# First group's four slabs side by side, the weights' bounds a group later, and the first output projection's rows landing in x's old buffer

## The chip, the cores and the metric

One core of a Trainium2 chip runs the whole program. The metric is the device time of one execution in microseconds, the median of several runs. Work is done by TensorE (PE, matrix products into PSUM), VectorE (DVE), ScalarE (ACT) and GpSimd (POOL); SyncE (SP) issues most DMAs, and GpSimd's queue issues some.

## What is computed

A trunk of two layers over 1024 tokens of width 1024. In layer 0 the main branch is a causal pooling in four groups, each with its own window and its own 256 x 256 map; beside it stands an attention into 256 memory tokens. Both are gated, and an output projection, a residual and a layer norm follow. Layer 1 (forgetting attention) is not touched by the change.

```python
def mixer_sublayer(x, mem, w_in, w_mem_kv, w_out, main_fn):
    h = x @ w_in                       # columns [main | mem q | main gate | mem gate]
    ...
    y_main = main_fn(u_main)           # layer 0: pooling, windows 2, 4, 8, 16
    y_mem = memory_attention(q_mem, mem, w_mem_kv)
    y = jnp.concatenate([y_main * jax.nn.silu(g_main), y_mem * jax.nn.silu(g_mem)], axis=-1)
    return y @ w_out
...
    x = layer_norm(ALPHA * x + y, ln_g[layer], ln_b[layer])
...
    # pooling: (trailing mean over the window - the token), then a map per group, then a scale
    mixed = jnp.einsum('bsgc,gcd->bsgd', pm, pool_w)
```

## The kernel before

x lies transposed in SBUF as eight tiles of 128 features by 1024 tokens. Each fp32 number is split in parts: `hi` (ScalarE's cast, fp32r), `lo` (what VectorE leaves of it, bf16) and `top` (a bf16 copy of the high part). A product of two such numbers is three matmuls (`three`): high x high, top x low, low x top. `X.top` is made by GpSimd, one copy per tile.

A *slab* is 128 columns of the input weights times all of x: 8 tiles of x, two halves of the tokens (n) and three parts, so 48 matmuls of 128 x 512. Its weights come in two pieces of 256 KB (`pc` 0 and 1, four tiles of x each). The first two slabs use `Wide` weights, whose low part is fp32r too, so that it can be multiplied with x's high part and needs no `X.top`.

Group 0 of the pooling is what the kernel starts with: slabs 0 and 1 (the pooled channels), then slabs 12 and 13 (their gates), then the group's map (L325, 24 matmuls), then the memory attention, then groups 1 to 3. Before the first weights are there, TensorE runs warm-up products on zeros (L98). `load_first` and `load_x` write the loads of the first weights and of x; `raw` is a ring of four landings for weights, `T` a ring of six tiles of 4 KB per partition, in which x lands and which later holds the pooled channels, the parts of mem and the rows of y. In PSUM, `pj` has two banks, `L` four and `T` two.

Most of the order on each engine is set when the program is built, by a scheduler that places instructions by its own costs; `keep_in_program_order` pins an instruction behind those pinned before it on its engine, and `manual_schedule` keeps TensorE's order as written.

`look_ahead` reads weights of layer 1 ahead of time, only to bound them: GpSimd's queue loads a piece into `W`, and VectorE (the first 12) or ScalarE sums its absolute values into `sums`. It is called every so many matmuls of slabs, 80 pieces in all, in group 0's gates, the memory queries, and groups 1 and 2. `bounds_of_weights` takes the maximum of `sums`, transposes it on TensorE (L297), reduces it on VectorE (L298, L299) and spreads it by a small matmul (L300).

`OutProj.rest` runs the output projection in twelve steps: four pairs of row blocks (sp), and in each three thirds (c = 2, 0, 1) of the 1536 inputs. A step loads a third of y's rows from DRAM (`y0d`, 512 KB) into a `T` tile, splits it into two further `T` tiles, and does 48 matmuls (L617). `lines` is a buffer of 32 KB per partition in the place where x's low and top parts were; the norm uses its rows 9 to 14, and `keep` its rows 5 to 8.

Of the kernel before, what the change touches and what calls it, by code (L numbers as in the profile page):

```python
# [9 lines left out]
F32 = mybir.dt.float32  # L10
F32R = mybir.dt.float32r
BF16 = mybir.dt.bfloat16
# [3 lines left out]
ALU = mybir.AluOpType  # L16
AX = mybir.AxisListType

P = 128
S = 1024  # L20
# [52 lines left out]
def run(units):  # L73
    for _ in units:
        pass
# [3 lines left out]
def trunk_kernel(ctx, tc, x, xT, memT, win, wk, wv0, wv, wmk, wmv, wout, poolw, pscale, lng, lnb, bforget, out):  # L79
# [14 lines left out]
    warm = pool.tile([P, NH], BF16, tag="w", name="warm", bufs=6)  # L94
    nc.vector.memset(warm, 0.0)
    idle = psum.tile([P, NH], F32, tag="L", name="idle", bufs=4)
    for _ in range(9):
        nc.tensor.matmul(idle, warm[:, :P], warm, start=True, stop=True)  # L98

    def nm(tag):  # L100
# [3 lines left out]
    def sb(shape, tag, bufs, dt=F32, where=None):  # L104
        return (where or pool).tile(shape, dt, tag=tag, name=nm(tag), bufs=bufs)
# [7 lines left out]
    def T(shape=(P, S), dt=F32R):  # L113
        return sb(list(shape), "T", 6, dt)
# [67 lines left out]
    def parts_of(make, shape):  # L182
        return Split(make(shape), make([shape[0], 2] + list(shape[1:]), BF16))
# [378 lines left out]
    class OutProj:  # L562
# [70 lines left out]
        def begin(self):  # L633
# [8 lines left out]
            for to, y in tiles:  # L642
                pin(nc.scalar.copy(to.top, y))

        def rest(self, resid, X, dst):
            order = [(sp, c) for sp in range(ST // 2) for c in (2, 0, 1)]
            accs, splits, gb = {}, [24], []
            if self.accs:
                accs[0], order[:6], splits = self.accs, [(0, 0), (1, 2), (0, 1), (1, 0), (1, 1)], [16, 24]
            if X is not None:  # L650
                self.split(splits.pop())

            def loads():

                for v in (lng, lnb):
                    t = sb([P, D], "P", 4)
                    nc.sync.dma_start(t, v[self.l].partition_broadcast(P))
                    gb.append(t)

            for sp, c in order:  # L660
                if c == 2:
                    accs[sp] = self.open((("T", 2), ("pj", 2), ("T", 2), ("L", 4))) if 0 in accs and sp == 1 else self.open()
                if self.begun and (sp, c) == (0, 0):
                    ys = self.begun
                else:
                    src, ys = T([P, 4, 2 * P], F32), parts_of(T, [P, 4, 2 * P])
                    nc.sync.dma_start(src, self.yd[c, :, :, sp * 2 * P : (sp + 1) * 2 * P])
# [63 lines left out]
    X = parts_of(stream, [P, KT, S])  # L731

    def load_x(kt, parts=1):
        r = T(dt=F32)
        for i in range(parts):
            cols = slice(i * S // parts, (i + 1) * S // parts)
            nc.sync.dma_start(r[:, cols], xT[kt, :, cols])
            nc.scalar.copy(X.hi[:, kt, cols], r[:, cols])
            nc.vector.tensor_tensor(X.lo[:, kt, cols], r[:, cols], X.hi[:, kt, cols].bitcast(F32), ALU.subtract)

    x1 = dram.tile([S, D], F32, name="x1")
    y0d = dram.tile([3, P, 4, S], F32, name="y0d")
# [2 lines left out]
    with tc.tile_pool(name="in0", bufs=1) as in0:  # L745

        def bt(shape=(P, S), dt=F32R):
            return sb(list(shape), "B", 8, dt, in0)

        def seen(shape):  # L750
            return sb(shape, "W", 4, F32, in0)

        first = [[], []]

        def load_first(f, pc):
            to, r = Wide(bt([P, 2, 4, P]), wt([P, 4, P], BF16)), raw([P, 4, P])
            nc.sync.dma_start(r, win[0, f, pc])
            hi_lo(to, r)
            first[f].append(to)

        load_first(0, 0)
        load_x(0, 2)
        load_first(1, 0)
        for kt in range(1, 4):
            load_x(kt)
# [12 lines left out]
        nc.vector.tensor_scalar(pschalf, psc, 0.5, None, ALU.mult)  # L778

        def pool_group(g, see=None):  # L780
            w = WINDOWS[g]
            pms = []
            for f in (2 * g, 2 * g + 1):
                u = sb([P, S], "P", 4)
                run(slab(
                    first[f] if g == 0 else win[0, f], X, lambda cols, acc: nc.scalar.copy(u[:, cols], acc),
                    ("L", 4) if f == 1 else ("pj", 2),
                ))
                cur, sh = u, 1
                while sh < w:  # L790
                    nxt = G()
                    nc.vector.tensor_tensor(nxt[:, sh:], cur[:, sh:], cur[:, : S - sh], ALU.add)
# [12 lines left out]
            ys = []  # L805
            for f in (2 * g, 2 * g + 1):
                y = sb([P, S], "Y", 4, F32, in0)
                if g == 0:
                    seeing[0] = see
# [599 lines left out]
```

## Time and profile before

| | us |
|---|---|
| runs shown | 1182.02, 1182.39, 1179.73; median 1182.02 |
| the profiled execution, its own time | 1181.94 |
| its span | 1180.2 |
| TensorE busy | 1160.1 (98%) |
| VectorE, ScalarE, GpSimd busy | 774.3, 677.7, 290.1 |

The span is the time from the first to the last instruction in the trace; the own time has what lies around it. All times in the trace count from the span's start. A busy TensorE may still run at half its clock, so the granted clock is to be read beside the busy time. Several instructions of one form that follow each other stand in one row of the order of time, with their count (x48); what is in brackets is the idle time ahead of the row and the instruction that ended it. A few matmuls are missing from the trace.

### The profile page before, as it was taken

What the parts mean: (1) busy time and instruction counts of PE and PEld (TensorE: products, weight loads), DVE (VectorE), ACT (ScalarE), POOL (GpSimd) and SP (SyncE); (2) the same over time, 40 slices, a digit from 0 to 9 for tenths busy, and PEclk for the clock granted to TensorE, in tenths of its full rate; (3) what the DMA queues carried; (4) which work ended last, traced back from release to release, by engine and by line L of the source; (5) the groups of instructions that cost most, each with busy time, mean ns of one, the idle gap of its engine ahead of it and who ended that gap; (6) DMA issues with size and microseconds to landing.
All of it is one profiled execution on the core that took longest, in us unless ns stands there. A gap on an engine that the chain in (4) does not pass through costs nothing. (4 is left out here: it accounts for less than half of the span.)

```text
span 1180.2 us, 20768 instructions
## 1 busy us (share of the span) xinstructions
PE 1160.1 (98%) x7398; PEld 671.8 (57%) x7445; DVE 774.3 (66%) x1827; ACT 677.7 (57%) x1502; POOL 290.1 (25%) x443
## 2 busy tenths in 40 slices
PE   8999999999999999999999999999999999999997
PEld 5566776555555556555674455555555555455554
DVE  6744675555765556547555877778777787784653
ACT  6478775966563233557521776667666677774120
POOL 3321001310000000000012445555554444760000
PEclk8999999999999999999999999999999999999999
DMA  7576657754375554536474879999999999965430
GB/s 262 169 247 198 160 118 215 227 192 152 89 256 166 155 136 117 143 89 124 94 250 106 174 161 227 209 211 199 195 207 161 185 195 196 236 190 175 149 137 36
DMA packets 286712, 203.96 MB, mean 173 GB/s; under 512 B 225168, under 2 KB 238608, under 8 KB 286608
## 3 DMA queue, kind: packets, MB, share of 16 engines
q1 hardware_dynamic: 279632, 179.49, 62.1%
q0 software_dynamic: 6976, 23.14, 6.1%
q8 instruction: 58, 0.95, 0.3%
q14 instruction: 46, 0.38, 0.1%
HBM read 116.01 MB, written 22.61 MB: 117 GB/s over the span
## 5 line engine op out<-in xcount | busy, mean ns | idle before, releaser
L361 PE MATMUL pj<-A,w 128*128 128x512 f16 (+2 forms) x2827 | 646.4, 383 | 3.9 <-DVE A L965 1.2
L361 PEld LDWEIGHTS <-w 128*128 128x128 f16 (+1 forms) x2560 | 247.1, 98 | 283.3 <-issue 12.4
L1088 ACT ACTIVATE T<-MK,s 128x512 f32<-128x512 f32 x192 | 111.2, 579 | 60.2 <-DVE s L1080 39.3
L1117 DVE SCALAR_TENSOR_TENSOR P<-T,s,P 128x512 f16<-128x512 f32 x192 | 112.3, 613 | 49.1 <-ACT P L1116 49.1
L1116 ACT ACTIVATE P<-T,s 128x512 f16<-128x512 f32 x192 | 103.8, 574 | 61.3 <-ACT T L1088 29.5
L617 PEld LDWEIGHTS <-T 128*128 128x128 bf16 x736 | 70.6, 98 | 88.7 <-issue 4.7
L1054 POOL TENSOR_SCALAR_AFFINE_SELECT raw<-R 128x256 f32<-128x256 f32 (+3 forms) x128 | 59.8, 468 | 191.2 <-DVE s L1080 133.5
L201 DVE TENSOR_TENSOR w<-raw,w 128x512 bf16<-128x512 f32 x74 | 52.5, 710 | 59.8 <-ACT w L200 40.1
L325 PE MATMUL L<-A 128*128 128x512 f16 (+3 forms) x384 | 83.8, 326 | 0.7 <-DVE G L1207 0.6
L558 POOL DMA_DIRECT2D y1d<-V x3 | 1.6, 535 | 334.8 <-DVE V L536 332.3
L361 PEld LDWEIGHTS pj<-A,w 128*128 128x128 f32 x352 | 65.1, 188 | 17.0 <-ACT w L200 1.4
L201 DVE TENSOR_TENSOR T<-T,T 128x1024 bf16<-128x1024 f32 x22 | 26.8, 1219 | 68.2 <-ACT T L200 39.4
L180 POOL TENSOR_TENSOR w<-B,w 128x512 f16<-128x512 f32 x54 | 62.8, 1163 | 4.4
L200 ACT CAST w<-raw 128x512 fp32r<-128x512 f32 x76 | 46.8, 615 | 24.8 <-DMA raw<-in_win_dram 10.9
L325 PEld LDWEIGHTS <-A 128*128 128x128 f16 x384 | 36.4, 98 | 42.6 <-issue 1.2
L200 ACT CAST T<-T 128x1024 fp32r<-128x1024 f32 x22 | 23.0, 1047 | 64.9 <-DMA T<-y1d 32.3
L617 PE MATMUL pj<-B,T 128*128 128x512 bf16 (+1 forms) x194 | 54.2, 385 | 0.2
L617 PE MATMUL L<-B,T 128*128 128x512 bf16 (+1 forms) x183 | 52.1, 393 | 0.2
L202 ACT CAST w<-raw 128x512 bf16<-128x512 f32 x78 | 48.2, 618 | 3.3 <-PE pj L361 1.9
L1080 DVE CUSTOM_DVE_ANT_0 MK<-L,R,scales 128x512 f32<-128x512 f32 x64 | 45.3, 709 | 2.2 <-PE L L325 2.0
L513 ACT ACTIVATE P<-L,s 128x256 f32<-128x256 f32 x64 | 29.5, 472 | 22.9 <-DVE s L510 19.5
L269 ACT ACTIVATE W<-W 128x512 f32<-128x512 f32 (+1 forms) x68 | 42.2, 624 | 0.0
(310 smaller groups left out, 1880.1 us busy)
## 6 DMA issues: line engine op xcount, KB each, us to landing
raw<-in_win_dram SPq DMA_DIRECT2D x66, 256.0 KB, 3.5
W<-in_win_dram POOLq DMA_DIRECT2D x48, 256.0 KB, 4.0
R<-cumd SPq DMA_DIRECT2D x16, 512.0 KB, 4.8
B<-in_win_dram SPq DMA_DIRECT2D x15, 512.0 KB, 5.6
y0d<-Y SPq DMA_DIRECT2D x12, 512.0 KB, 4.0
raw<-in_wout_dram SPq DMA_DIRECT2D x24, 256.0 KB, 2.7
T<-y0d SPq DMA_DIRECT2D x12, 512.0 KB, 4.9
A<-A SPq DMA_DIRECT2D x24, 256.0 KB, 4.0
```

What stands on the lines that cost most here:

```text
L180: pin(nc.gpsimd.tensor_tensor(to.lo, src, to.hi, ALU.subtract))
L200: pin(nc.scalar.copy(to.hi, src))
L201: pin(nc.vector.tensor_tensor(to.lo, src, to.hi.bitcast(F32), ALU.subtract))
L202: pin((top or nc.scalar.copy)(to.top, src))
L325: nc.tensor.matmul(acc, a, b, start=i == 0, stop=i == len(terms) - 1)
L361: nc.tensor.matmul(accs[n], a[:, k, :], b[:, pc * 4 + k, n * NH : (n + 1) * NH], start=seen[n] == 1, stop=seen[n] == 3 * KT,)
L617: nc.tensor.matmul(accs[a][nh], y, w, start=kt == 8 and i == 0, stop=kt == 7 and i == 2,)
L1054: tc.keep_in_program_order(nc.gpsimd.affine_select(C[:, :w], R[:, lo:up], [[-1, w]], ALU.is_ge, -NEG, base=w - P, channel_multiplier=1,))
L1080: tc.keep_in_program_order(nc.vector.tensor_tensor_reduce(p[:, lo:up], lg, rows, unq, top, ALU.add, ALU.min, m[:, n : n + 1]))
L1088: nc.scalar.activation(e, p[:, lo:up], AF.Exp, bias=top, scale=-1.0, accum_out=sums[:, n, hd % 2, i : i + 1],)
L1116: nc.scalar.activation(pair[:, lo:up], e, AF.Copy, scale=r)
L1117: nc.vector.scalar_tensor_tensor(pair[:, L + lo : L + up], e, r, pair[:, lo:up], ALU.mult, ALU.subtract)
```

## The change

Four things. Group 0's four slabs are computed side by side by `first_four`, in an order written out by hand: as a tile of x arrives, the wide products of slabs 0 and 1 and the high products of the gates are done with it; the products with x's low and top parts follow when all of x is there. All eight PSUM banks are used for it. The weight pieces of the gates are loaded between x's tiles, the loads and splits are pinned in that order, and the `top` copies of these weights come behind all of them. `bounds_of_weights` moves from the end of group 2 into group 3, ahead of its map. From the second step on, the first output projection loads y's rows into rows 0 to 3 of `lines` (`landing`) instead of a `T` tile. There are ten warm-up products instead of nine.

```diff
-    for _ in range(9):
+    for _ in range(10):
         nc.tensor.matmul(idle, warm[:, :P], warm, start=True, stop=True)
...
+        def landing(self, sp, c):
+            k = 2 * ((sp + c) % 2)
+            return lines[0][:, k : k + 2, :].bitcast(F32).rearrange("p e (k m) -> p (e k) m", k=4 // 2)
...
-                    src, ys = T([P, 4, 2 * P], F32), parts_of(T, [P, 4, 2 * P])
+                    src = T([P, 4, 2 * P], F32) if X is None or (sp, c) == (0, 2) else self.landing(sp, c)
+                    ys = parts_of(T, [P, 4, 2 * P])
...
-        def load_first(f, pc):
-            to, r = Wide(bt([P, 2, 4, P]), wt([P, 4, P], BF16)), raw([P, 4, P])
-            nc.sync.dma_start(r, win[0, f, pc])
-            hi_lo(to, r)
-            first[f].append(to)
+        def load_first(k, pc):
+            r, pin = raw([P, 4, P]), tc.keep_in_program_order
+            if k < 2:
+                to = Wide(bt([P, 2, 4, P]), wt([P, 4, P], BF16))
+            else:
+                if pc == 0:
+                    splits[k] = bt([P, 2, 4, P]), bt([P, 2, 2, 4, P], BF16)
+                to = Split(*(half[:, pc] for half in splits[k]))
+            pin(nc.sync.dma_start(r, win[0, (0, 1, 12, 13)[k], pc]))
+            pin(nc.scalar.copy(to.hi, r))
+            pin(nc.vector.tensor_tensor(to.lo, r, to.hi.bitcast(F32), ALU.subtract))
+            firsts[k, pc] = to
...
+        def first_four(us, ys, see):
+            tags = (("pj", 2), ("L", 4), ("L", 4), ("T", 2))
...
+            def wide(kt):
+                for k in range(2):
+                    for i in (0, 2):
+                        for n in range(2):
+                            product(k, kt, n, i)
+            def high(k, *kts):
+                for kt in kts:
+                    for n in range(2):
+                        product(k, kt, n, 0)
+            wide(0)
+            wide(1)
+            high(2, 0, 1)
+            for kt in (2, 3):
+                wide(kt)
+                high(2, kt)
+            high(3, 0, 1, 2, 3)
+            wide(4)
+            wide(5)
+            high(2, 4, 5)
+            wide(6)
+            high(2, 6)
+            wide(7)
+            high(2, 7)
+            high(3, 4, 5, 6, 7)
+            for k in range(2):
+                for n in range(2):
+                    for kt in range(KT):
+                        product(k, kt, n, 1)
+            seeing[0] = see
...
+            for k in range(2, 4):
+                for n in range(2):
+                    for i in (1, 2):
+                        for kt in range(KT):
+                            product(k, kt, n, i)
+                            done += 1
+                            if done % 7 == 0:
+                                look_ahead()
 
         load_first(0, 0)
         load_x(0, 2)
         load_first(1, 0)
-        for kt in range(1, 4):
-            load_x(kt)
-        for f in range(2):
-            load_first(f, 1)
-        for kt in range(4, KT):
-            load_x(kt)
+        load_x(1)
+        load_first(2, 0)
+        load_x(2)
+        load_x(3)
+        load_first(3, 0)
+        for k in range(4):
+            load_first(k, 1)
+            load_x(4 + k)
+        for to in firsts.values():
+            tc.keep_in_program_order(nc.scalar.copy(to.top, to.hi.bitcast(F32)))
...
+            if g == 3:
+                bounds_of_weights()
             for d in range(2):
...
-            if g == 2:
-                bounds_of_weights()
```

Three places in the built order show it. The first is TensorE's start, right behind the warm-up products. The names: `pj` and `L` are PSUM banks, `A_110` (before) and `A_111` (after) x's high part, `B` the weights of a slab. Before:

```order
L361 MATMUL pj_202<-A_110,B_118 128x512 [waits Activation_49]
L361 MATMUL pj_207<-A_110,B_118 128x512 [waits Activation_49]
L361 MATMUL L_267<-A_110,B_132 128x512 [waits Activation_49]
L361 MATMUL L_272<-A_110,B_132 128x512
L361 MATMUL pj_202<-A_110,B_118 128x512 [waits Activation_49]
```

After:

```order
L783 MATMUL pj_232<-A_111,B_120 128x512 [waits Activation_49]
L783 MATMUL pj_233<-A_111,B_120 128x512 [waits Activation_49]
L783 MATMUL pj_232<-A_111,B_120 128x512 [waits DVE_49]
L783 MATMUL pj_233<-A_111,B_120 128x512
L783 MATMUL L_234<-A_111,B_133 128x512 [waits Activation_49]
L783 MATMUL L_235<-A_111,B_133 128x512
L783 MATMUL L_234<-A_111,B_133 128x512 [waits DVE_49]
```

The low products of slab 0 with x's tile 0 now stand ahead of slab 1, where only its high ones stood. The second place is SyncE's queue around the first output projection's loads of y (`y0d` is read into a tile, and written from `Y`). Before:

```order
L667 DMA T_3420<-y0d 128x4x256 [waits DMAHW7_49,PE_49]
L583 DMA raw_3375<-in_wout_dram 128x512 [waits DMAHW0_49,DMAHW1_49,DVE_49,Activation_49]
...
L583 DMA raw_3399<-in_wout_dram 128x512 [waits DMAHW5_49,DVE_49,Activation_49]
L657 DMA P_3427<-in_lng_dram 128x1024
...
L822 DMA y0d<-Y_3237 128x1024 [waits DMAHW2_49,DVE_49]
L667 DMA T_3479<-y0d 128x4x256 [waits PE_49]
```

After:

```order
L672 DMA T_3420<-y0d 128x4x256 [waits PE_49]
L583 DMA raw_3375<-in_wout_dram 128x512 [waits DMAHW0_49,DMAHW1_49,DVE_49,Activation_49]
...
L672 DMA A_3341<-y0d 128x4x256 [waits PE_49,Pool_49]
L583 DMA raw_3399<-in_wout_dram 128x512 [waits DMAHW5_49,DVE_49,Activation_49]
L661 DMA P_3427<-in_lng_dram 128x1024
...
L899 DMA y0d<-Y_3225 128x1024 [waits DVE_49]
```

The second load of y (`T_3479` before, `A_3341`, which is `lines`, after) has moved from behind the last store of y to ahead of a weight load. The third place is TensorE around the bounds of the weights. Before, at the end of group 2's map:

```order
L297 MATMUL T_2928<-ident,s_2925 3x128 [waits PE_49]
L361 MATMUL pj_2993<-A_110,w_2988 128x512 [waits DVE_49]
L361 MATMUL pj_2993<-A_110,w_2988 128x512 x3
L361 MATMUL pj_2993<-A_110,w_3000 128x512 [waits Activation_49]
L361 MATMUL pj_2993<-A_110,w_3000 128x512
L300 MATMUL T_2928<-s_2927,ones 128x3 [waits DVE_49]
```

After, ahead of group 3's map:

```order
L297 MATMUL T_3297<-ident,s_3294 3x128 [waits PE_49]
L325 MATMUL L_3306<-T_3056,MK_3151 128x512
...
L325 MATMUL L_3306<-T_3145,MK_3152 128x512
L300 MATMUL T_3297<-s_3296,ones 128x3 [waits DVE_49]
```

The two small products have moved to the start of group 3's map. Elsewhere TensorE's order is the same in both.

More of the change, by code (lines that the diff above doesn't have):

```diff
@@ L733, in load_x @@
     def load_x(kt, parts=1):
-        r = T(dt=F32)
+        r, pin = T(dt=F32), tc.keep_in_program_order
         for i in range(parts):
             cols = slice(i * S // parts, (i + 1) * S // parts)
-            nc.sync.dma_start(r[:, cols], xT[kt, :, cols])
-            nc.scalar.copy(X.hi[:, kt, cols], r[:, cols])
-            nc.vector.tensor_tensor(X.lo[:, kt, cols], r[:, cols], X.hi[:, kt, cols].bitcast(F32), ALU.subtract)
+            pin(nc.sync.dma_start(r[:, cols], xT[kt, :, cols]))
+            pin(nc.scalar.copy(X.hi[:, kt, cols], r[:, cols]))
+            pin(nc.vector.tensor_tensor(X.lo[:, kt, cols], r[:, cols], X.hi[:, kt, cols].bitcast(F32), ALU.subtract))
     x1 = dram.tile([S, D], F32, name="x1")
@@ L751, in seen @@
             return sb(shape, "W", 4, F32, in0)
-        first = [[], []]
-        def load_first(f, pc):
-            to, r = Wide(bt([P, 2, 4, P]), wt([P, 4, P], BF16)), raw([P, 4, P])
-            nc.sync.dma_start(r, win[0, f, pc])
-            hi_lo(to, r)
-            first[f].append(to)
+        firsts, splits = {}, {}
+        def load_first(k, pc):
[10 more added lines that the diff above has]
+            firsts[k, pc] = to
@@ new lines, in first_four, with product @@
+        def first_four(us, ys, see):
+            tags = (("pj", 2), ("L", 4), ("L", 4), ("T", 2))
+            accs = [[ps([P, NH], *tag) for _ in range(2)] for tag in tags]
+            seen_of = {}
+            def product(k, kt, n, i):
+                a, b = three(firsts[k, kt // 4], X)[i]
+                cols = slice(n * NH, (n + 1) * NH)
+                at = seen_of[k, n] = seen_of.get((k, n), 0) + 1
+                nc.tensor.matmul(
+                    accs[k][n], a[:, kt % 4, :], b[:, kt, cols], start=at == 1, stop=at == 3 * KT,
+                )
+                if at == 3 * KT and k < 2:
+                    nc.scalar.copy(us[k][:, cols], accs[k][n])
+                elif at == 3 * KT:
+                    gate(accs[k][n], ys[k - 2][:, cols])
+            def wide(kt):
[27 more added lines that the diff above has]
+            seeing[0] = see
+            done = 0
+            for k in range(2, 4):
[6 more added lines that the diff above has]
+                                look_ahead()
@@ L782, in pool_group @@
             pms = []
-            for f in (2 * g, 2 * g + 1):
[L784 to L788, printed above, removed]
+            us = [sb([P, S], "P", 4) for _ in range(2)] if g == 0 else []
+            ys = [sb([P, S], "Y", 4, F32, in0) for _ in range(2)] if g == 0 else []
+            if g == 0:
+                with tc.manual_schedule(engines={PE}):
+                    first_four(us, ys, see)
+            for f in (2 * g, 2 * g + 1):
+                u = us.pop(0) if g == 0 else sb([P, S], "P", 4)
+                if g:
+                    run(slab(win[0, f], X, lambda cols, acc: nc.scalar.copy(u[:, cols], acc)))
                 cur, sh = u, 1
@@ L804, in pool_group @@
             hi_lo(w2, r)
-            ys = []
-            for f in (2 * g, 2 * g + 1):
+            for f in (2 * g, 2 * g + 1) if g else ():
                 y = sb([P, S], "Y", 4, F32, in0)
-                if g == 0:
-                    seeing[0] = see
                 run(gate_units(win[0, 12 + f], y, X))
                 ys.append(y)
+            if g == 3:
+                bounds_of_weights()
             for d in range(2):
```

## The prediction

> **What bounds the kernel now.** I read the page first: the span, the busy share of each engine, then the waits of TensorE over the whole span, and then the stretches of the start in time.
>
> ```profile
> span 1180.2 us, 20768 instructions
> PE 1160.1 (98%) x7398; PEld 671.8 (57%) x7445; DVE 774.3 (66%) x1827; ACT 677.7 (57%) x1502; POOL 290.1 (25%) x443
> ...
> PE pj L361 <- ACT A L738: 1.3, 2, 1.0
> PE L L361 <- ACT B L200: 1.1, 1, 1.1
> PE L L617 <- ACT T L202: 0.9, 1, 0.9
> ```
>
> TensorE is busy in 98% of the span, so only two things can move the time: its few idle microseconds and the stretches in which it runs slowly. The three waits quoted are those that this change touches first: 1.3 and 1.1 us for x and for weights at the start, 0.9 us in the first output projection (L617). The first group also runs slowly, which busy time hides. Five stretches of 3.41 us, cut where the granted clock changes, show it (columns: busy us and matmuls of TensorE, granted clock, DMA share, GB/s), and below them TensorE in order of time:
>
> ```profile
> 1.39:4.80 3.41, 3.41 (x9) 1.00 0.85 256
> 4.80:8.21 3.41, 1.95 (x6) 1.00 0.98 357
> 8.21:11.62 3.41, 2.43 (x7) 0.50 1.03 408
> 11.62:15.04 3.42, 3.42 (x10) 0.50 1.03 413
> 15.04:18.45 3.41, 3.41 (x17) 1.00 1.02 375
> ...
> 5.45 1.02 PE L361 MATMUL pj<-A,B 128*128 128x512 f32 x2 [0.34 <-ACT A L738]
> 9.28 1.22 PE L361 MATMUL pj<-A,B 128*128 128x512 f32 x2 [0.98 <-ACT A L738]
> 11.15 1.05 PE L361 MATMUL pj<-A,B 128*128 128x512 f32 x2
> 12.00 1.05 PE L361 MATMUL L<-A,B 128*128 128x512 f32 x2
> 55.09 4.20 PE L325 MATMUL L<-T,MK 128*128 128x512 f32 x17
> 60.35 10.90 PE L361 MATMUL pj<-A,w 128*128 128x512 f32 x48
> 71.09 4.08 PE L412 MATMUL pj<-T,w 128*128 128x256 f32 x35
> ```
>
> The reader is to see three things. The slab that starts at 60.35 runs undisturbed: 48 matmuls until 71.09, so 0.224 us each. At the half clock two start every 0.85 us (11.15 to 12.00), so 0.427 us each. And the first group, four slabs of 48 and the 24 matmuls of L325, lasts from 5.45 to 60.35, 54.9 us, where four slabs at 10.74 and the 5.26 from 55.09 to 60.35 make 48.2. So 6.7 us are lost there: 2.1 us to the waits for weights (1.1) and for x's tile 1 (0.98), 5.76 x (1 - 0.224 / 0.427) = 2.7 us to the half clock from 9.28 to 15.04, and the rest to pauses too short to be listed as waits.
>
> **Part 1: four slabs side by side.** What TensorE waits for is ScalarE's cast of what has just landed:
>
> ```profile
> 6.89 0.62 ACT L200 CAST B<-raw 128x512 fp32r<-128x512 f32 x1 [0.98 <-DMA raw<-in_win_dram]
> 8.18 1.04 ACT L738 CAST A<-T 128x1024 fp32r<-128x1024 f32 x1
> 9.46 1.04 ACT L738 CAST A<-T 128x1024 fp32r<-128x1024 f32 x1 [0.24 <-DMA T<-in_xT_dram]
> 10.76 1.05 ACT L738 CAST A<-T 128x1024 fp32r<-128x1024 f32 x1 [0.26 <-DMA T<-in_xT_dram]
> 17.23 1.06 ACT L738 CAST A<-T 128x1024 fp32r<-128x1024 f32 x1 [0.24 <-DMA T<-in_xT_dram]
> 7.54 0.69 DVE L201 TENSOR_TENSOR B<-raw,B 128x512 fp32r<-128x512 f32 x1 [0.82 <-ACT B L200]
> ```
>
> Tiles of x (512 KB) land 1.30 us apart (9.46, 10.76), so a weight piece of 256 KB costs 0.65. The order of the first loads up to x's tile 1 is kept; then four gate pieces come in between, so tile 2 lands at 10.1, tile 3 at 11.4, tile 4 (behind two pieces) at 14.0, and tile 7 at 17.23 + 4 x 0.65 = 19.8. Add 1.05 for each cast.
>
> TensorE then: the first four products of slab 0 start at 5.45 as before and use the gap up to 7.5; slab 1 has its weights at 7.51 and their low part at 8.23; tile 1 is cast at 9.22. By then 8 products are through, and from 9.22 on 184 slab products and 24 of the pooling map are left. At the full clock that is 184 x 0.224 + 5.26 = 46.4 us, the end 55.65. No input is late from here on: tile 2 is first needed 12 products after 9.22 (11.9, at the full clock) and ready at 11.15; tile 3 needed at 14.1 and ready at 12.45; tile 7 needed 70 products after 9.22, at 24.9 or later, ready at 20.9. Every tile now feeds 12 products instead of 8, which is what closes the gap.
>
> The clock is the unknown. In the rows above, the stretch with 1.95 us busy of 3.41 is followed by the half clock, the one with 2.43 us (71%) leaves it there, and only the full one lifts it. After the change 4.80:8.21 holds at most two more products, some 60%, so I let the clock fall at 8.21 again. But 8.21:11.62 is then filled from 8.23 to 9.09 and from 9.22 on, 3.26 us of 3.41, nearer to the full stretch than to 71%: I take it that the clock is back at 11.62. From 9.22 to 11.62 then run 5.6 products instead of 10.7, 1.14 us late: **end 56.8, gain 3.55 us**. Both ends: the clock never falls, 55.65 (gain 4.7); it comes back only at 15.04, 13.6 products instead of 26, 2.77 us late, 58.4 (gain 1.9).
>
> The Trainium skill, "TensorE: Matmul & The Clock Gate", section "Part 1: The HAM clock gate (the "warmup" mystery)", says that the clock halves after an idle window of about 3.4 us, and that the windows are free-running. The trace agrees on the length (8.21 less 4.80) but not on the idleness: the longest wait here is 1.1 us. By the rule as worded the clock would not fall, which is the 55.65 above.
>
> The rest of the part costs nothing on TensorE, for these reasons. The tenth warm-up product runs in the 0.34 us gap before 5.45. Four more pieces add 4 x 0.52 to ScalarE and 4 x 0.6 to VectorE, which both wait for landings there. ScalarE's eight top casts move behind the last landing, 20.9 to 25.1; they are first needed after the 96 high and wide products, at 9.22 + 1.14 + 88 x 0.224 = 30.1. GpSimd's copies of x's top hang on tile 6:
>
> ```profile
> 18.45 1.17 POOL L195 TENSOR_SCALAR s<-A 128x1 f32<-128x1 bf16 x1 [17.09 <-DVE pschalf L778]
> 19.59 4.95 POOL L195 TENSOR_SCALAR A<-A 128x1024 bf16<-128x1024 f32 x4
> 27.45 5.04 POOL L195 TENSOR_SCALAR A<-A 128x1024 bf16<-128x1024 f32 x4
> 27.01 4.59 DVE L792 TENSOR_TENSOR G<-P 128x1023 f32<-128x1023 f32 x1
> 37.85 1.22 DVE L792 TENSOR_TENSOR G<-P 128x1023 f32<-128x1023 f32 x1 [0.61 <-ACT P L786]
> ```
>
> They end 14 us after they start, so at 34.3 if they start at 20.2; the gates want them one by one from 39 on. The pooling sums of VectorE start when slab 0 is out, after 34, so they should take the 1.22 us of the lower row and not the 4.59 us of the upper, which ran beside these copies. Both pooled channels are then split by about 46, and the map wants them at 51.5.
>
> **Part 2: rows of y in x's old buffer.** SyncE's load of the second step waits for a free T, behind weight loads and stores in its queue:
>
> ```profile
> 318.90 9.11 SPq L583 DMA_DIRECT2D raw<-in_wout_dram  x5
> 337.01 0.53 SPq L667 DMA_DIRECT2D T<-y0d  x1
> 335.69 0.62 ACT L200 CAST MK<-raw 128x512 fp32r<-128x512 f32 x1 [1.47 <-DMA raw<-in_wout_dram]
> 343.60 1.04 ACT L200 CAST T<-T 128x1024 fp32r<-128x1024 f32 x1 [1.57 <-DMA T<-y0d]
> 345.65 0.60 PE L617 MATMUL L<-W,T 128*128 128x512 bf16 x2 [0.88 <-ACT T L202]
> ```
>
> The load is issued at 337.01, cast at 343.6, and TensorE stands 0.88 us. With the new buffer it waits only for the last slab's products that read x's low half, and it stands in front of the fifth of the weight loads of the first row, which end at 328.0. Its casts come right behind the weight pair cast from 335.69 on, at about 337 to 339, and TensorE wants them at 344.8. **Gain 0.9** (bounds 0 and 0.9). The later steps share two landings, three steps in a row on one, so a load waits for the casts before it; a step's 48 products take 10.6 us, and a landing of 6.6 us plus 2.2 us of casts fits. No step but the second waits in that stage before the change.
>
> **Part 3: bounds a group later.** Before, the small product L300 waits for VectorE, which has other sums ahead of it:
>
> ```profile
> 285.07 0.27 PE L297 MATMUL T<-ident,s 128*3 128x128 f32 x1
> 287.13 0.38 PE L300 MATMUL T<-s,ones 3*128 3x3 f32 x2 [0.41 <-DVE s L299]
> 286.56 0.27 DVE L298 TENSOR_REDUCE s<-T 3x1 f32<-3x128 f32 x1
> 286.86 0.22 DVE L299 TENSOR_SCALAR s<-ident,s 3x3 f32<-3x3 f32 x1
> ```
>
> Now it stands behind five products of group 3's map, 1.1 us, against 0.27 + 0.22 of VectorE, before that map's own sums. **Gain 0.3** (0 to 0.4). The twelve looks into the weights become nine in group 0; the three others go to group 2's spare places.
>
> **Sum:** 3.55 + 0.9 + 0.3 = 4.75 us. The profiled execution took 1181.94 us (its span and 1.7 us around it), which stands 0.08 below the median of the three runs, 1182.02. So 1181.94 - 4.75 = 1177.2.
>
> **The rivals.** *The clock comes back only at 15.04.* For it: it did in this execution. Then 1.9 + 0.9 + 0.3 = 3.1, and 1178.8. *The clock never falls*, because 4.80:8.21 is busier, or because the boundaries lie elsewhere in another execution: 4.7 + 1.2 = 5.9, and 1176.0. *The change does not do what it says*: the four slabs run, but landings are later than their bytes say (gate pieces wait for the raw ring, whose four slots hang on VectorE), and the out projection still waits. If tile 7 were cast at 28.5 and not 20.9, TensorE, there at 26.0 (70 products after 9.22 and the 1.14 us), would lose 2.5 us of part 1; with nothing from part 2 that leaves 1.05 + 0.3, and 1180.6. Against it: VectorE frees the slot of slab 1's first piece at 8.23 (the row at 7.54), and tile 7 has 5 us to spare.
>
> *On the other side: the weights of the first memory-query slab come too late.* Before, their casts were
>
> ```profile
> 46.94 3.27 SPq L214 DMA_DIRECT2D raw<-in_win_dram  x2
> 54.08 0.62 ACT L200 CAST w<-raw 128x512 fp32r<-128x512 f32 x1 [7.31 <-DMA raw<-in_win_dram]
> 56.11 0.62 ACT L200 CAST w<-raw 128x512 fp32r<-128x512 f32 x1 [0.39 <-DMA raw<-in_win_dram]
> ```
>
> 5.7 us ahead of 60.35. Now TensorE is there at 56.8, and the load waits for the casts of mem, which stand behind those of the pooled channels: I put its issue at 46.5, its cast with the same 7.1 us at 54.2, so 2.6 us are left. Each microsecond beyond that is lost one for one; 7.4 us later than I think the gain is gone, and from 9.7 us on the kernel is slower by 0.2%, 1184.4. It would need VectorE's pooling sums to take 4.59 us each once more.
>
> **How the numbers follow.** A difference under 0.2% (2.4 us) can hardly be told from none here; the three runs shown spread over 2.7 us. Chances: my forecast 0.55; clock back late 0.18; never down 0.10; does not do what it says 0.12; weights late 0.05. The first three are faster by over 0.2%: 0.83. The fourth and a little of the fifth make no difference that can be told, 0.13; the rest of the fifth is slower, 0.04. The range reaches from the best clock, 1176.0 less 0.8 of spread between runs, to the rival of 1180.6 plus 0.6 of the same spread: 1175.2 to 1181.2, and leaves out the late weights and some of the fourth.
>
> **What would show it.** Right: the first slab products back to back from 9.2, clock 1.00 from 11.6, the first matmul of the memory queries (L361) near 56.8; no wait of L617 for a cast of T; no wait at L300. Wrong: the clock at 0.50 up to 15 (part 1's size); waits for x after 9.3 (landings); a wait of L361 for a cast of w near 57 (the weights); pooling sums of 4.6 us on VectorE; L617 waiting still near 340.

## The result and the profile after

The changed kernel takes 1174.86 us at the median of 6 runs (1174.46 to 1175.85). The kernel before, timed beside it, came to 1180.33, and its 68 runs in the whole study have the same median, 1180.33 (1177.80 to 1183.01). Three slow executions of the study (1503.19, 2026.65 and 6931.10 us) are left out of every median. The ratio is 0.995, with a 95% interval of 0.9938 to 0.9963: 5.5 us faster, where 4.75 had been forecast, and 0.34 us below the low end of the range.

The head of the page of the changed kernel, and the first of TensorE's waits over its span (total, times, longest, in us):

```profile
span 1172.9 us, 20813 instructions
PE 1158.6 (99%) x7446; PEld 671.6 (57%) x7446; DVE 770.0 (66%) x1827; ACT 680.0 (58%) x1502; POOL 288.2 (25%) x443
```

```profile
PE pj L783 <- ACT A L743: 1.7, 2, 1.4
```

The waits of L361 for B, of L617 for T and of L300 are gone. The longest wait for x was 1.0 us, for tile 1; it is now 1.4 us, for the second half of x's first tile. The stretches between the possible changes of the clock (busy us and matmuls of TensorE, granted clock, DMA share, GB/s), and below them TensorE in order of time at the start and at the end of the first group:

```profile
5.10:8.51 3.41, 1.97 (x8) 1.00 0.98 348
8.51:11.92 3.41, 3.15 (x13) 1.00 1.03 411
11.92:15.34 3.42, 3.42 (x16) 1.00 1.02 398
```

```profile
5.12 0.58 PE L783 MATMUL pj<-A,B 128*128 128x512 f32 x1
7.14 0.97 PE L783 MATMUL pj<-A,B 128*128 128x512 f32 x3 [1.44 <-ACT A L743]
7.94 1.34 PE L783 MATMUL L<-A,B 128*128 128x512 f32 x4
9.54 1.19 PE L783 MATMUL pj<-A,B 128*128 128x512 f32 x4 [0.26 <-ACT A L743]
10.57 2.02 PE L783 MATMUL L<-A,B 128*128 128x512 f32 x8
...
50.64 4.38 PE L325 MATMUL L<-T,MK 128*128 128x512 f32 x18
...
56.02 10.97 PE L361 MATMUL pj<-A,w 128*128 128x512 f32 x48
```

The granted clock stays at 1.00 after 5.10, though the stretch 5.10:8.51 is hardly busier (1.97 us) than the one of 1.95 us after which it fell before. From 9.54 on products run without a listed wait, and the first memory query starts at 56.02 instead of 60.35. That is 4.33 us of the 7.29 us between the two profiled executions (1181.94 and 1174.65; the first of them stood 1.6 us above its kernel's median). The rest comes later, 1.21 us of it up to the start of the output projection (333.69 and 328.15). The places of the other two parts look like this now:

```profile
322.44 0.27 PE L297 MATMUL T<-ident,s 128*3 128x128 f32 x1
...
323.55 0.38 PE L300 MATMUL T<-s,ones 3*128 3x3 f32 x2
...
320.97 0.53 SPq L672 DMA_DIRECT2D A<-y0d  x1
329.96 1.05 ACT L200 CAST T<-A 128x1024 fp32r<-128x1024 f32 x1
339.00 0.59 PE L617 MATMUL L<-W,T 128*128 128x512 bf16 x2
```

The load of the second step is issued at 320.97, ahead of most of the weight loads, and cast 8 us before L617 reads it. Here the two traces stand 6.65 us apart (345.65 and 339.00).

### The profile page after: what moved, and what is told of

It reads as the page before. It is cut to its first block, busy times and chain, and to the rows that moved or that the text cites. A ratio compares the mean times of both kernels' runs of the same rounds, so it can differ in the third digit from the quotient of the medians.

```text
span 1172.9 us, 20813 instructions
## 1 busy us (share of the span) xinstructions
PE 1158.6 (99%) x7446; PEld 671.6 (57%) x7446; DVE 770.0 (66%) x1827; ACT 680.0 (58%) x1502; POOL 288.2 (25%) x443
## 5 line engine op out<-in xcount | busy, mean ns | idle before, releaser
L361 PE MATMUL pj<-A,w 128*128 128x512 f16 (+2 forms) x2736 | 620.7, 382 | 1.9 <-DVE A L1040 1.0
L361 PEld LDWEIGHTS <-w 128*128 128x128 f16 (+1 forms) x2464 | 238.5, 98 | 270.5 <-issue 7.9
L617 PEld LDWEIGHTS <-T 128*128 128x128 bf16 x736 | 70.6, 98 | 87.5 <-issue 4.1
L201 DVE TENSOR_TENSOR w<-raw,w 128x512 bf16<-128x512 f32 x70 | 48.2, 689 | 51.1 <-ACT w L200 35.4
L361 PEld LDWEIGHTS pj<-A,w 128*128 128x128 f32 x320 | 59.5, 188 | 13.7
L617 PE MATMUL pj<-B,T 128*128 128x512 bf16 (+1 forms) x198 | 54.8, 384 | 0.0
L617 PE MATMUL L<-B,T 128*128 128x512 bf16 (+1 forms) x186 | 52.4, 393 | 0.0
L202 ACT CAST w<-raw 128x512 bf16<-128x512 f32 x70 | 43.4, 620 | 2.9 <-PE pj L361 1.5
L1155 DVE CUSTOM_DVE_ANT_0 MK<-L,raw,s 128x512 f32<-128x512 f32 (+1 forms) x64 | 41.1, 643 | 0.5 <-issue 0.3
L412 PE MATMUL pj<-T,w 128*128 128x256 bf16 (+1 forms) x344 | 41.0, 279 | 0.0
```

Of the source, the lines that this page charges most:

```text
L201: pin(nc.vector.tensor_tensor(to.lo, src, to.hi.bitcast(F32), ALU.subtract))
L202: pin((top or nc.scalar.copy)(to.top, src))
L361: nc.tensor.matmul(accs[n], a[:, k, :], b[:, pc * 4 + k, n * NH : (n + 1) * NH], start=seen[n] == 1, stop=seen[n] == 3 * KT,)
L617: nc.tensor.matmul(accs[a][nh], y, w, start=kt == 8 and i == 0, stop=kt == 7 and i == 2,)
L1155: tc.keep_in_program_order(nc.vector.tensor_tensor_reduce(p[:, lo:up], lg, rows, unq, top, ALU.add, ALU.min, m[:, n : n + 1]))
```

## The experiments

The table sums them up. "Less before" is the median less that of the kernel before in the same set of runs, and "products a tile" are those of slabs 0 and 1 that are done when a tile of x comes. "Products" are TensorE's products of the first group that have started by 15.04 us in the profile (about one record of them is missing from each trace). "Query" is the start of the first memory-query product, all in us.

| kernel | median | less before | products | query |
|---|---|---|---|---|
| before (profile 1) | 1180.33 | 0 | 18 | 60.35 |
| before, profile 2 | | | 16 | 61.33 |
| changed | 1174.86 | -5.47 | 32 | 56.02 |
| first part alone | 1175.29 | -5.13 | 34 | 55.51 |
| landing alone | 1179.53 | -0.89 | 23 | 59.15 |
| bounds alone | 1179.39 | -1.03 | 21 | 59.35 |
| landing and bounds | 1179.20 | -0.47 | 18 | 59.84 |
| before, 20 warm-ups | 1179.95 | -0.47 | 25 | 59.52 |
| changed, 2 warm-ups | 1175.68 | -4.44 | 31 | 56.24 |
| changed, 9 warm-ups | 1175.51 | -4.61 | 29 | 56.67 |
| 8 products a tile, gates behind | 1175.15 | -4.97 | 34 | 55.47 |
| 4 products a tile, gates behind | 1178.28 | -1.84 | 19 | 58.92 |
| 8 products a tile, gates as before | 1179.07 | -0.61 | 32 | 60.08 |

**The first part alone.** The changed kernel without its other two parts:

```
-                    src = T([P, 4, 2 * P], F32) if X is None or (sp, c) == (0, 2) else self.landing(sp, c)
+                    src = T([P, 4, 2 * P], F32)
...
-            if g == 3:
-                bounds_of_weights()
...
+            if g == 2:
+                bounds_of_weights()
```

> The first part alone: four slabs side by side with the tenth warm-up product, while the second step's rows of y land in T as before and the bounds stay at the end of group 2. Theory C (the granted clock, which stayed at 1.00 in the changed kernel, and the gap-free first slabs make the start's gain, and the start makes most of the whole): the first memory-query product starts near 56.0 us instead of 60.35, as in the changed kernel; from the marks of the two traces 4.3 us by the end of group 0 and 5.2 us by group 3, so 1 to 1.5 us slower than the changed kernel, near 1176.2, if the kernel before is at its median of 1180.3. Rival S (the record's split): 3.55 of 4.75 us from this part, the rest from the other two. Rival N (the parts depend on each other: SyncE's queue and the sums of VectorE move together): the marks behind group 3 differ from the changed kernel's by more than the 1.1 us of the out projection and the 0.36 us of the bounds.

Ratio 0.9955 (0.9943 to 0.9968), 1175.29 us. So the first part brings 5.1 us of 5.5, more than theory C's 4.1 and than the prediction's share of 3.55 in 4.75. What the other two add is 0.43 us, less than the spread of either kernel's runs (1.4 and 1.5), so it is not shown to differ from nothing. TensorE's row of the second output step, where rows of y still land in T:

```profile
338.68 0.60 PE L617 MATMUL L<-W,T 128*128 128x512 bf16 x2
```

No wait stands behind it, although its load is issued as late as 329.89: the 0.88 us that the second part was to save is not there in this profile.

**The landing alone and the bounds alone**, each put into the kernel before:

```
+        def landing(self, sp, c):
...
-                    src, ys = T([P, 4, 2 * P], F32), parts_of(T, [P, 4, 2 * P])
+                    src = T([P, 4, 2 * P], F32) if X is None or (sp, c) == (0, 2) else self.landing(sp, c)
```

> The kernel before with the second part alone: rows of y land in x's old buffer instead of T. By the record: 0.9 us faster (0 to 0.9), the wait of L617 for the cast of T gone near 345. By the marks of the two traces: 1.1 us by the first output row and up to 0.5 us more over layer 1 if that later gain hangs on this landing too, so 0.9 to 1.6 us faster than the kernel before. Rival: the first group has to be faster for the load to be issued earlier; then L617 still waits and the time does not move.

```
+            if g == 3:
+                bounds_of_weights()
...
-            if g == 2:
-                bounds_of_weights()
```

> The kernel before with the third part alone: the bounds of the weights are taken inside group 3. By the record 0.3 us faster (0 to 0.4), the wait of L300 at 287 gone. Rival: the sums then wait elsewhere on VectorE and group 3's map starts later by as much, 0. Nothing else may differ, so at the median within 0.5 us of the kernel before.

Ratios 0.9993 (0.9985 to 1.0002) and 0.9991 (0.9982 to 1.0): 0.9 and 1.0 us, each at the edge of what can be told from nothing. In the bounds' profile L617 does not wait for T either, though nothing was done about it there. The two together, and a second profile of the unchanged kernel, tell more.

> The kernel before with the second and the third part together, without the first. If the two are worth what each gave alone (0.9 and 1.0 us against 27 runs of the kernel before), 1178.4 to 1178.6 for a kernel before of 1180.3. If each took away a wait that comes and goes with the timing of the start, and they overlap: 0.9 to 1.2 us, 1179.2 to 1179.5. If they are worth what they add to the first part (1175.29 to 1174.86): 0.4 us, 1179.9.

Together 0.9992 (0.9983 to 1.0002), 0.5 us at the medians: they do not add up to 1.9, and the nearest of the three forecasts is the last, 0.4.

> The kernel before, unchanged, profiled a second time, to see what of its profile belongs to that execution. If the waits that the second and the third part are to take away are fixed: L617 again waits 0.9 us for the cast of T near 345, and L300 0.4 us near 287. If they come and go: one or both are absent, and the span is 1 to 2 us shorter than 1180.2. The first products again come four to a tile, and 18 to 25 are through by 15 us, whatever the clock does.

TensorE at the two places in the second profile of the unchanged kernel:

```profile
287.21 0.38 PE L300 MATMUL T<-s,ones 3*128 3x3 f32 x2
344.59 0.59 PE L617 MATMUL L<-W,T 128*128 128x512 bf16 x2
```

Neither waits (before: 0.41 and 0.88), and the execution took 1180.80 us. Nor do they stand in the other profiles that leave these places as they were: none of L617 for T in the first part alone, the bounds alone and 20 warm-ups, none of L300 in the first part alone, the landing alone and 20 warm-ups. Both waits belonged to the execution that I had read, and hardly to the kernel.

**The clock held in the old order.** 20 warm-up products instead of 9 in the kernel before:

```
-    for _ in range(9):
+    for _ in range(20):
```

> The kernel before with 20 warm-up products instead of 9, so that TensorE is busy about 2.4 us longer at full clock before the first product of x. Theory C: the granted clock then does not fall at 8.21; of the 2.7 us that the half clock cost in the profiled run the kernel gains what is left after the first products start 1 to 2 us later, so 0.7 to 1.7 us faster, with the end of group 0 at 58.7 to 59.7 instead of 60.35. Theory O (the order, 12 products for a tile, is what counts, and the clock falls or costs little): the start is 1 to 2 us later and the time 0 to 1.5 us longer than before.

Ratio 0.9991 (0.9982 to 1.0), 0.5 us. The clock rose at 6.02 and stayed at 1.00, as theory C asked, and the query starts at 59.52. TensorE:

```profile
9.53 0.73 PE L361 MATMUL pj<-A,B 128*128 128x512 f32 x2 [0.52 <-ACT A L738]
10.10 0.63 PE L361 MATMUL L<-A,B 128*128 128x512 f32 x2
10.80 0.73 PE L361 MATMUL pj<-A,B 128*128 128x512 f32 x2
11.37 0.63 PE L361 MATMUL L<-A,B 128*128 128x512 f32 x2
12.12 0.74 PE L361 MATMUL pj<-A,B 128*128 128x512 f32 x2
...
43.09 1.19 PE L361 MATMUL pj<-A,w 128*128 128x512 f32 x4 [1.00 <-DVE Y L378]
```

Each tile of x brings two products of slab 0 here (pj) and two of slab 1 (L). The rows of slab 0 start 1.27 and 1.32 us apart, as the tiles land, and not 0.9 us apart, as four products take at the full clock. So with four products a tile the old order starves at the full clock; at the half clock four products take 1.7 us and it does not. That is one reason why the half clock cost it so little. The other stands in the last row: TensorE is at the first gate slab at 31.35, 1.67 us earlier than before (33.02), and then loses 1.00 us in a wait for VectorE ahead of the second, where 0.18 us was lost before. In the profile of the bounds alone the clock rose only at 13.42; there the first gate slab starts at 32.20, the wait for VectorE is not listed, and the query starts at 59.35, no later than here.

Theory C's place for the query, 58.7 to 59.7, holds; its 0.7 to 1.7 us of time are not shown, with 0.5 us and an interval that reaches nothing. Theory O forecast 0 to 1.5 us of loss, and there is none: the 20 products, which put off the first product of x from 5.45 to 7.73, delayed nothing in the end.

**The clock taken from the new order.** The changed kernel with 2 and with 9 warm-up products instead of 10 (`range(10)` becomes `range(2)`, `range(9)`):

> The changed kernel with 2 warm-up products instead of 10, so that the first products of x run at the half clock. In the six profiles so far a stretch of 3.41 us was followed by the full clock when the equivalent of at least 6.1 products of 512 columns streamed in it, and by the half clock when 5.4 or fewer did. By that rule the clock rises here at the end of the first stretch that holds 6 products, between 9 and 12.5 us, as the tiles keep TensorE streaming at half clock from about 7 on. Theory O (feeding is what counts; at half clock TensorE is the limit with 12 products for a tile): 1 to 2.5 us of products are put off, the first memory-query matmul near 57 to 58.5, 1 to 2.5 us slower than the changed kernel (1174.9). Theory C (the clock explains the whole gain of the start): the loss is 4 us or more and the time is back at that of the kernel before, about 1179 to 1180.

> The changed kernel with 9 warm-up products, as before. If the tenth does nothing but fill a gap: the same time as the changed kernel, 1174.9, within 0.3 us, with the clock held by the 6 to 8 products in the stretch from about 5 to 8.4. If the tenth is what holds the clock: the clock is at 0.50 for 3.4 or 6.8 us, and the time is 1 to 2 us longer in the runs in which it falls.

0.9964 (0.9952 to 0.9977) and 0.9964 (0.9951 to 0.9976). The median is 0.8 and 0.65 us above the changed kernel's, the first just below theory O's 1 to 2.5 and far from theory C's 4, the second between the two forecasts of 0.3 and 1. With 9, the profile shows one fall (stretches, then TensorE's first memory query):

```profile
3.99:7.40 3.41, 1.60 (x7) 1.00 1.00 342
7.40:10.81 3.41, 3.41 (x10) 0.50 1.03 410
```

```profile
56.67 10.95 PE L361 MATMUL pj<-A,w 128*128 128x512 f32 x47
```

A fall of 3.41 us moves the query from 56.02 to 56.67, by 0.65 us in this one pair of profiles. With 2 warm-up products the clock came back at 9.86, once the tiles fed TensorE, and the query starts at 56.24, earlier than theory O's 57. Even such a cold start costs only about a sixth of the gain, so theory C falls: a clock held through the start is not what made it.

**Eight products a tile and four, gates behind.** Both load as the kernel before does, with the gates' pieces last, and run the gate slabs' products after slabs 0 and 1:

```
-            wide(0)
-            wide(1)
-            high(2, 0, 1)
...
+            for kt in range(KT):
+                wide(kt)
...
+            high(2, *range(KT))
+            high(3, *range(KT))
```

> The changed kernel, but the gate slabs come behind: the loads are in the order of the kernel before with the gates' pieces last, and a tile of x feeds 8 products (hi and low weights of slabs 0 and 1) when it comes, not 12. By the record, 12 products for a tile close the gap, so 8 would leave it partly open: 1 to 2 us slower than the changed kernel. Theory F, from the new traces: in the kernel before a tile feeds only 4 products when it comes (0.9 us of work for a landing every 1.3 us), since the low weights follow after four tiles; 8 are 1.7 us of work for 1.3 us and are enough: within 0.4 us of the changed kernel, 1174.5 to 1175.3, with pairs of products back to back from tile 1 on.

0.9961 (0.9947 to 0.9974), 1175.15 us, 0.3 us above the changed kernel, as theory F said. TensorE goes from tile to tile:

```profile
8.93 1.20 PE L783 MATMUL pj<-A,B 128*128 128x512 f32 x4 [0.27 <-ACT A L743]
9.97 1.08 PE L783 MATMUL L<-A,B 128*128 128x512 f32 x4
10.89 1.10 PE L783 MATMUL pj<-A,B 128*128 128x512 f32 x4
```

The tiles start 1.96 us apart (8.93, 10.89), slower than they land: TensorE is the limit. Twelve products for a tile are not needed. With four, in the old order of slabs 0 and 1:

```
-            for kt in range(KT):
-                wide(kt)
+            for four in (range(4), range(4, KT)):
+                for kt in four:
+                    for k in range(2):
+                        high(k, kt)
+                for k in range(2):
+                    for n in range(2):
+                        for kt in four:
+                            product(k, kt, n, 2)
```

> As the two-by-two kernel, but slabs 0 and 1 take their products in the order of the kernel before: four high products for a tile, the low weights after each four tiles; the gates still side by side behind them. Theory F: TensorE starves 0.4 us a tile at the full clock or runs at the half clock, and is 6 to 11 products behind the changed kernel at 15 us, as the kernels with the old order were (18 to 25 products then against 32 and 34): 1.3 to 2.4 us of the gain lost here, the rest kept, since the waits for the gates' results near 43 us are gone: 1176.2 to 1177.4. Theory G (nothing of the gain comes from the first tiles, all of it from the gates side by side): as the changed kernel, 1174.9. Theory T (all of it comes from the first tiles): as the kernel before but for the other two parts, 1178.5 to 1180.

0.9984 (0.9975 to 0.9992), 1178.28 us. That is 3.1 us slower than with eight: theory F's cause, with a size 0.9 us above its range, since the kernel was 15 products behind at 15 us (19 to 34) and not 6 to 11; theory T's 1178.5 is as near as theory F's 1177.4. Fifteen products of 0.22 us are 3.3 us, and the query is 3.45 us later (58.92 to 55.47). The stretches show what the products were lost to:

```profile
4.07:7.49 3.42, 1.84 (x7) 1.00 0.97 322
7.49:10.90 3.41, 2.92 (x6) 0.50 1.02 407
10.90:14.31 3.41, 3.41 (x9) 0.50 1.03 409
```

With so few products for a tile the clock fell at 7.49 and stayed at 0.50 up to 14.31, while with eight it stayed at 1.00 from 6.16 on. So the 3.1 us are the price of starving and of the half clock that follows from it; no run parts the two in this kernel. With the clock held, the old order had 25 products through and not 34.

**Eight products a tile, gates as before.** If the first tiles were all, slabs 0 and 1 side by side would do:

```
-            tags = (("pj", 2), ("L", 4), ("L", 4), ("T", 2))
+            tags = (("pj", 2), ("L", 4))
...
-            for f in (2 * g, 2 * g + 1) if g else ():
+            for f in (2 * g, 2 * g + 1):
```

(and without the gates' loads and products in `first_four`)

> The changed kernel, but only slabs 0 and 1 are written side by side with 8 products for a tile, with the loads of the kernel before; the two gate slabs follow as they did before, with their own loads. Theory F (a tile must feed more work than a landing takes; 8 products do): 32 to 34 products through by 15 us. If the gates side by side are worth nothing: the time of the two-by-two kernel, 1175.1. If TensorE, now 3 us earlier at the gates, meets the wait for VectorE's gate results that was 1.0 us near 43 in the kernel with 20 warm-up products: 1 to 3 us of the gain is lost there, 1176.2 to 1178.2, with a wait of L361 for Y near 41 to 43 of that size.

0.9992 (0.9983 to 1.0001), 1179.07 us: nearly all of the gain is gone. TensorE, VectorE and GpSimd there in order of time, and the stretches of the clock:

```profile
29.42 10.96 PE L361 MATMUL pj<-A,w 128*128 128x512 f32 x48
42.58 12.48 PE L361 MATMUL pj<-A,w 128*128 128x512 f32 x48 [2.20 <-DVE Y L378]
...
27.02 4.77 DVE L845 TENSOR_TENSOR G<-P 128x1023 f32<-128x1023 f32 x1
...
40.40 1.22 DVE L201 TENSOR_TENSOR T<-G,T 128x1024 bf16<-128x1024 f32 x1 [0.52 <-ACT T L200]
41.84 0.69 DVE L378 SCALAR_TENSOR_TENSOR Y<-Y,pj 128x512 f32<-128x512 f32 x1 [0.21 <-ACT Y L377]
...
27.64 5.05 POOL L195 TENSOR_SCALAR A<-A 128x1024 bf16<-128x1024 f32 x4
```

```profile
39.82:43.24 3.42, 1.22 (x6) 1.00 0.23 77
43.24:46.65 3.41, 3.41 (x10) 0.50 0.52 173
```

The same two slabs in the kernel before:

```profile
33.02 10.74 PE L361 MATMUL pj<-A,w 128*128 128x512 f32 x47
43.95 11.30 PE L361 MATMUL pj<-A,w 128*128 128x512 f32 x47 [0.18 <-DVE Y L378]
```

TensorE is at the first gate slab at 29.42, 3.6 us earlier than before. The second gate slab needs an accumulator of the pair pj, which VectorE empties at 41.84, behind its pooling sums (the first of 4.77 us beside GpSimd's copies) and ScalarE's casts of them: 1.4 us earlier than before (43.21), for a TensorE that is 3.6 us earlier. TensorE stands 2.20 us. In that stretch it is busy for 1.22 us, the clock falls, and 3.41 us at the half clock cost half of them, 1.7 us more. 2.20 and 1.7 make 3.9, against the 3.3 us that are lost of the lead (3.6 us at 29.42, 0.27 at the query, 60.08 to 60.35); the rest, 0.6 us, is what the old order itself loses at the gates, where its two slabs take 22.1 us (33.02 to 55.09) and not 2 x 10.74. The expectation allowed for the wait, not for the fall of the clock behind it.

The two halves of the first part thus need each other. With the other two parts in place, eight products a tile alone give 0.6 us, the gates side by side alone 1.8, both 5.0. Side by side, the four gate halves have banks of their own (tags L and T), and none of them shows a wait for VectorE.

## Why the prediction was wrong

*The base.* "1181.94 - 4.75 = 1177.2" failed first. The profiled execution stood 0.08 us below the median of the three runs shown, but only five of the 68 runs took 1181.9 us or more, and two of these five are among the three shown; the median of all is 1180.33. That was the bad luck of a small sample, but the spread allowed at the low end, 0.8 us, came from the same three runs and did not cover it. From 1180.33 the same 4.75 gives 1175.6 and the low end 1173.6, and the result lies inside.

*Part 1.* The direction was right, the size too small: 3.55 forecast, 5.1 measured (4.33 at the first query of the profiles). The term that was mis-sized is the clock's: 1.14 us were taken off for a fall that did not come. Without it the working had the query at 55.65, a gain of 4.7, and the first part alone showed it at 55.51. Two steps of the reasoning were wrong besides, though they did not enter the sum. "Every tile now feeds 12 products instead of 8, which is what closes the gap": before, a tile fed 4 when it came, since the low weights followed after four tiles; 8 are enough (1175.15 us), 4 are not (1178.28). The working also gave the gates side by side no price of their own, because the wait that they avoid is only 0.18 us before (43.95); it becomes 2.20 us, with a clock fall behind it, for a TensorE that arrives earlier. What would be late next was asked for the weights of the query alone.

*The clock.* "4.80:8.21 holds at most two more products, some 60%, so I let the clock fall": the stretch came out at 58% and the clock held. The rival "never falls" had 0.10 and came true; busy time was the wrong measure. Of the "2.7 us" put down to the half clock before, holding it with 20 warm-ups gave back 1.67 at the first gate slab and 0.5 in time, since the old order then waits for tiles and for VectorE. Where it falls in the new order it cost 0.65 us for one stretch, against 1.14 forecast.

*x's first tile.* "the first four products of slab 0 start at 5.45 as before and use the gap" is half right: one started at 5.12, and the other three waited 1.44 us, since the second half of tile 0 was cast at 6.47. The profiled execution of the kernel before was the exception here too: in the twelve other profiles, of either order, that half is cast between 5.83 and 6.68. ScalarE's cast of that half, its cast of the query's weights, and VectorE's first pooling sum:

```profile
6.47 0.62 ACT L743 CAST A<-T 128x512 fp32r<-128x512 f32 x1 [1.65 <-DMA T<-in_xT_dram]
...
49.39 0.62 ACT L200 CAST w<-raw 128x512 fp32r<-128x512 f32 x1 [3.07 <-DMA raw<-in_win_dram]
...
34.38 1.23 DVE L870 TENSOR_TENSOR G<-P 128x1023 f32<-128x1023 f32 x1 [1.31 <-ACT P L787]
```

*Parts 2 and 3.* "Gain 0.9" and "Gain 0.3" were read from waits that the second profile of the kernel before does not have. The waits are gone as forecast, but the time they are worth is 0.4 to 0.5 us together, not shown to differ from nothing. That the total of 4.75 came within 0.7 us of the measured 5.47 is partly luck: part 1 was forecast 1.6 us too small and these two 0.7 to 0.8 us too large.

*What held.* The query's weights are cast at 49.39 (forecast 54.2), 6.6 us ahead of 56.02, so the rival on the other side had no ground. The first pooling sum took 1.23 us and not 4.59. Tile 7 was through its cast at 21.25 (forecast 20.9), so late landings, the rival of 1180.6, played no part either.

It remains open whether parts 2 and 3 are worth anything in time, how much of the price of four products a tile is starving and how much the half clock, and why the old kernel's runs spread over 5 us and the new one's six over 1.4. That this spread comes from where the start falls in the stretches of the clock is a guess.

## What to carry to other kernels

Where inputs land one by one, count what one landing feeds at once and set it against the time between landings: 0.9 us of products for 1.3 us starve TensorE or let its clock fall, 1.8 us do not, and more bought nothing here. Before counting a gain at one place, ask what the engine meets next when it comes 3 us earlier; a wait of 0.18 us may be the edge of one of 2.2. And one profile shows one execution: waits under a microsecond should be seen in a second one before they are priced.

## What the runs showed of the hardware

The stretches of 3.41 us do not start with the program. With 9 or 10 warm-ups, all starting at 1.25, the clock rose anywhere from 3.99 to 6.29, and once, where the warm-ups straddled a boundary, only at 13.42. The Trainium skill, "TensorE: Matmul & The Clock Gate", "Part 1: The HAM clock gate (the "warmup" mystery)", calls the windows free-running; these runs agree. The same section of the Trainium skill puts the fall after an idle window; here it came after stretches in which TensorE was busy up to 1.95 us.

What separates the cases is not busy time but how many products stream in a stretch. Worked out from the starts of the records (0.216 us a product at the full clock and 0.427 at the half, products across a boundary by their share):

```
stretch (kernel)                        clock in it   products   clock after
4.80:8.21   (before)                    1.00          4.6        0.50
39.82:43.24 (8 a tile, gates as before) 1.00          4.1        0.50
6.29:9.70   (landing alone)             1.00          5.0        0.50
4.07:7.49   (4 a tile)                  1.00          5.6        0.50
7.49:10.90  (4 a tile)                  0.50          5.5        0.50
2.87:6.29   (landing alone)             0.50          6.1        1.00
5.10:8.51   (changed)                   1.00          6.9        1.00
```

Ahead of a trace's first record of the clock, as in 2.87:6.29 (and in 1.39:4.80 of the kernel before), the view of the stretches writes 1.00; the products there start 0.427 us apart, so 0.50 is put here. In all 13 profiles each stretch of the start fits a bound between 5.6 and 6.1 products of 512 columns, whether the clock was up or down. It is worked out from this kernel's products alone; what the chip counts was not shown.
